# Low parts of the first weight quad: parts 1 and 2 subtracted on VectorE, parts 3 to 7 still made by an accumulating transfer

## The chip, the cores and the metric

The kernel runs on one core of a Trainium2 chip. The metric is device time in microseconds (us) of one execution, and the figure for the kernel before is the median of three runs: 1482.7 us (1477.24 to 1484.63). Beside these runs stands one profiled execution, from which every duration below is read.

A core has five engines that work at the same time, each through its own queue of instructions in order: TensorE (PE in the profile; PEld is its weight load), VectorE (DVE), ScalarE (ACT), GpSimd (POOL) and SyncE (SP). The last two only issue transfers here. An instruction that has to wait for another engine or for a transfer holds up everything behind it in its own queue.

## The reference

Two layers of an encoder over 512 positions of width 1024, in float32. Each layer has an attention half and a feed-forward half:

```python
for l in range(DEPTH):                        # DEPTH = 2
    h = rms_norm(x, attn_norm_g[l])
    z = jnp.einsum('bsd,dc->bsc', h, w_in[l])
    ...                                       # split, RoPE, two attention branches, gates
    x = x + jnp.einsum('bsd,de->bse', mixed, w_out[l])
    h = rms_norm(x, ffn_norm_g[l])
    u = jax.nn.silu(jnp.einsum('bsd,df->bsf', h, w_gate[l])) * jnp.einsum('bsd,df->bsf', h, w_up[l])
    x = x + jnp.einsum('bsf,fd->bsd', u, w_down[l])
```

The case lies in the feed-forward half: `w_gate` and `w_up` are 1024 x 2816, `w_down` is 2816 x 1024.

## The kernel before

**Numbers in two parts.** A float32 matrix is held as a rounded high part `h` (type fp32r) and a low part `lo = src - h`. A product takes three matmuls: high by high, high by low, low by high. So each operand of TensorE needs two preparations. ACT makes the high part (`A.copy`, in the profile CAST). The low part is made in one of two ways: VectorE subtracts (`V.tensor_tensor(..., ALU.subtract)`), or ACT writes `-h` (in the profile ACTIVATE) and POOL issues a transfer that adds the source to it (`accum_op=ALU.add`).

**The feed-forward half.** 256 columns of `w_gate` and `w_up` are taken straight (`pair_matmul`); the other 2560 go in five groups of 512 columns ("quads"), each quad as seven products of 512-row halves in place of eight (Strassen's scheme). A quad's source arrives as two raw tiles, `a11, a21` and `a12, a22`, each quarter 128 x 4 x 256. The seven parts are needed in the order 1, 5, 6, 2, 7, 3, 4 (`ORDER`, line 466). Part 1 is `a11`, part 2 is `a12`; parts 5, 6, 7 and 3 are sums that `Quad.high` makes on VectorE, most of them in place: for part 6 it overwrites `a21` and then `a11`, for part 3 it overwrites `a12`. The input has seven parts of the same kind, made once a layer by `chain_x` (lines 1360 to 1405): `high` on ACT, `low` on VectorE, and sums on VectorE between them.

**Where the first quad lies.** The first quad of `w_gate` of each layer (q = 0) is prepared early, while the last products with `w_out` and the straight columns still run. For it alone `by_transfer` is true (set in line 491, read in line 578): its seven low parts are made by ACT and POOL (`low_by_transfer`, lines 532 to 535). All later quads subtract on VectorE.

**One step of TensorE and what it needs.** `m_step` (line 1459) runs 24 matmuls of 256 columns for one part. After part 1, `seed` (line 1479) lets ACT copy the result to another bank; the matmuls of part 6 add to that bank, so TensorE can't begin part 6 before the copy is done. `evac_g` and `evac_u` (lines 1413 and 1419) take the straight columns out of the accumulators: VectorE scales, ACT applies SiLU, VectorE multiplies, ACT and VectorE split the result in two parts.

**What sets the order.** The kernel is planned before it is built: a dry pass walks through it with a clock per engine and estimated durations, and fixes the order in which each queue gets its instructions. Weight work falls due at positions counted in TensorE's time (`at_pos`, `tick`); other work stands in chains that are advanced when their operands are estimated to be ready (`Need`, `issue`). The same pass notes when each buffer is first and last used, and `Layout.pack` lays all buffers into two arenas (float32 and fp32r) so that buffers share room when their uses don't meet. An instruction that overwrites a buffer waits until everybody has read it, transfers included.

In the rows that follow `arena_72` is the float32 arena, `arena_73` the fp32r arena, `mm` and `at` are accumulator banks. Every instruction goes through one helper, so all have line 308 and are told apart by engine, operation, names and shape.

Of the kernel before, what the change touches and what calls it, by code (L numbers as in the profile page):

```python
# [213 lines left out]
def trunk(ctx: ExitStack, tc: tile.TileContext, a: dict, out: bass.AP, lay: Layout):  # L214
# [20 lines left out]
    def buf(shape, dtype=F32):  # L235

        n = int(np.prod(shape))
        x = lay.place(n, dtype)
        t = arenas[dtype][:, x : x + n]
        if len(shape) == 2:  # L240
            t = t.rearrange("p (a b) -> p a b", b=shape[1])
        elif len(shape) == 3:
            t = t.rearrange("p (a b c) -> p a b c", b=shape[1], c=shape[2])
        return t
# [287 lines left out]
    def low_by_transfer(lo, src, h):  # L532

        A.activation(lo, h.bitcast(F32), AF.Copy, scale=-1.0)
        GQ.dma_start(lo, src, accum_op=ALU.add)

    class Quad:
# [37 lines left out]
        def low(self, m):  # L575
            src, h = self.parts[m]
            lo = buf([4, 256], F32R)
            if self.by_transfer:
                low_by_transfer(lo, src, h)
            else:  # L580
                V.tensor_tensor(lo, src, h.bitcast(F32), ALU.subtract)
            self.parts[m] = h, lo
# [503 lines left out]
    def layer(l):  # L1086
# [273 lines left out]
        def chain_x():  # L1360
# [26 lines left out]
            high(1, b11)  # L1387
            V.tensor_tensor(n1, b11, b12, ALU.subtract)
            yield from low(1)
            high(5, n1)  # L1390
            yield from normal(1)
            V.scalar_tensor_tensor(n2, n1, -1.0, b22, ALU.mult, ALU.subtract)
            high(6, n2)
            yield from low(5)
            yield from low(6)
            high(2, b21)
            yield from low(2)
# [194 lines left out]
```

## Time and profile before

| | |
|---|---|
| median of 3 runs | 1482.7 us (1477.24 to 1484.63) |
| the profiled execution's own time | 1478.58 us |
| its span, first to last instruction | 1476.8 us |
| mean granted TensorE clock | 0.983 |
| busy, share of the span | PE 95%, DVE 62%, ACT 48%, POOL 25% |

A row of the timeline reads: start in us from the span's start, duration in us, engine, line, operation, output<-input with partitions x elements and types, how many such instructions follow each other, and in brackets the idle time of the engine just before it and what ended it. A row that joins several instructions shows the shape of the first. The view of waits adds up idle time by engine and releaser: total, how often, the longest. The chain of waits is followed back from the last instruction to what released it; "issue" is time in which the engine waited for nothing that the profile shows. In the table by windows, the value behind the busy times is the granted TensorE clock (1.00 is full), then the mean busy share of the DMA engines and GB/s.

### The profile page before, as it was taken

The page shows a single profiled execution, that of the slowest core. Times are in us where ns is not written, and L with a number is a line of the kernel's source. Part 1 is how long each engine was busy: PE and PEld are TensorE (multiplying, and loading weights), DVE is VectorE, ACT ScalarE, POOL GpSimd, SP SyncE. Part 2 cuts the span into 40 slices and gives each one's busy share as a digit, 9 for nine tenths or more (in the row PEclk, how much of TensorE's full clock was granted, in tenths as well). Part 3 has the DMA queues.
Part 4 walks back from the last instruction along what each step waited for, and adds up shares of the span by engine and source line. Part 5 has one row for each costly group of instructions (what it writes and reads, how often), then busy time and mean ns, then how long its engine had stood idle before and what let it go on. Part 6 is the DMA issues. An engine that isn't in the chain of part 4 may idle for free.

```text
span 1476.8 us, 21019 instructions
## 1 busy us (share of the span) xinstructions
PE 1405.2 (95%) x8074; PEld 1230.7 (83%) x8074; DVE 908.5 (62%) x1743; ACT 713.9 (48%) x1200; POOL 368.6 (25%) x374
## 2 busy tenths in 40 slices
PE   5999989999969999999999999999997999999998
PEld 4778878888869999999987887788886899999997
DVE  3876768543747565575647868673437575575653
ACT  3476657543544343433545775574345444343431
POOL 4533222234221110201353322123332211101111
PEclk9999999999989999999999999899999899999999
DMA  9877778899975745645798679669997754836455
GB/s 228 164 145 137 145 128 150 153 191 241 174 150 119 174 115 143 158 100 117 154 189 168 125 132 158 124 122 183 209 242 130 160 124 122 190 83 168 115 100 114
DMA packets 211427, 223.18 MB, mean 151 GB/s; under 512 B 25964, under 2 KB 179744, under 8 KB 211328
## 3 DMA queue, kind: packets, MB, share of 16 engines
q0 software_dynamic: 159920, 167.23, 61.1%
q1 hardware_dynamic: 51408, 54.62, 13.3%
q8 instruction: 63, 1.03, 0.3%
q14 instruction: 36, 0.29, 0.1%
HBM read 207.13 MB, written 2.10 MB: 142 GB/s over the span
## 4 chain that ended last, share of the span: by engine, by line
PE 69%; DMA 9%; DVE 9%; issue 7%; ACT 4%; POOL 2%; DVEq 0%; POOLq 0%; ACTq 0%; SPq 0%
PE mm L308 50%; PE at L308 19%; DVE arena L308 6%; ACT arena L308 4%; DMA arena<-arena 3%; DMA arena<-in_w_out 2%; DVE sm L308 2%; POOL arena L308 2%; DMA arena<-in_w_gate 1%; DMA arena<-in_w_up 1%; DMA arena<-in_rel_bias_b 1%; DMA vec<-in_q_norm_b 1%; DMA arena<-in_w_in 0%; ACT L308 0%; DVE hf L308 0%
## 5 line engine op out<-in xcount | busy, mean ns | idle before, releaser
L308 PE MATMUL mm<-arena 128*128 128x512 f32 (+1 forms) x5568 | 1127.9, 358 | 32.0 <-ACT mm L308 24.9
L308 PEld LDWEIGHTS mm<-arena 128*128 128x128 f32 x5568 | 910.1, 191 | 161.7 <-ACT mm L308 25.3
L308 PE MATMUL at<-arena 128*128 128x256 f32 (+2 forms) x1952 | 309.4, 299 | 15.1 <-DMA arena<-arena 12.3
L308 ACT ACTIVATE arena<-arena 128x1024 fp32r<-128x1024 f32 (+3 forms) x280 | 235.9, 865 | 176.9 <-DMA arena<-in_w_down 62.2
L308 ACT CAST arena<-arena 128x1024 fp32r<-128x1024 f32 (+2 forms) x250 | 211.7, 864 | 224.0 <-DVE arena L308 219.5
L308 PEld LDWEIGHTS at<-arena 128*128 128x128 f32 x1952 | 268.7, 193 | 38.7 <-DMA arena<-arena 11.9
L308 DVE TENSOR_TENSOR arena<-arena,arena 128x1024 fp32r<-128x1024 f32 (+2 forms) x236 | 228.3, 981 | 57.3 <-ACT arena L308 57.1
L308 POOL DMA_DIRECT2D arena<-in_w_in x168 | 168.4, 1367 | 368.3 <-ACT arena L308 367.9
L308 DVE TENSOR_TENSOR arena<-arena,mm 128x512 f32<-128x512 f32 x144 | 98.8, 686 | 255.9 <-PE mm L308 255.8
L308 POOL DMA_DIRECT2D arena<-in_w_down x96 | 98.2, 1210 | 503.2 <-ACT arena L308 388.4
L308 DVE TENSOR_TENSOR arena<-arena 128x1024 f32<-128x1024 f32 (+3 forms) x196 | 158.8, 824 | 19.2 <-DMA arena<-arena 14.1
L308 DVE TENSOR_TENSOR arena<-at,arena 128x384 fp32r<-128x384 f32 (+4 forms) x206 | 114.1, 562 | 52.7 <-ACT arena L308 45.9
L308 ACT CAST arena<-at 128x384 fp32r<-128x384 f32 (+2 forms) x164 | 74.4, 459 | 117.5 <-PE at L308 105.1
L308 PE MATMUL at<-cst,arena 128*128 128x128 f32 x504 | 87.4, 280 | 11.8 <-DVE arena L308 7.9
L308 PEld LDWEIGHTS at<-cst,arena 128*128 128x128 f32 x504 | 64.5, 143 | 30.5 <-DVE arena L308 10.9
L308 ACT ACTIVATE arena<-arena,negm 128x256 f32<-128x256 f32 (+1 forms) x128 | 71.6, 561 | 13.1 <-DVE negm L308 12.7
L308 DVE TENSOR_TENSOR arena<-mm,arena 128x512 f32<-128x512 f32 x72 | 49.3, 687 | 45.8 <-PE mm L308 45.7
L308 ACT COPY arena<-at 64x512 f32<-64x512 f32 (+1 forms) x60 | 34.8, 581 | 64.8 <-PE at L308 64.3
L308 POOL DMA_DIRECT2D arena<-in_w_out x32 | 35.2, 1292 | 54.5 <-ACT arena L308 54.5
L308 DVE CUSTOM_DVE_ANT_0 arena<-at,arena 128x256 f32<-128x256 f32 (+1 forms) x64 | 31.0, 486 | 28.7 <-PE at L308 28.4
L308 DVE CUSTOM_DVE_ANT_0 arena<-at,cst,nsnk 128x256 f32<-128x256 f32 (+1 forms) x64 | 34.3, 546 | 16.3 <-PE at L308 15.9
L308 DVE TENSOR_SCALAR arena<-arena,sm 128x384 f32<-128x384 f32 (+1 forms) x97 | 34.0, 405 | 1.1
(70 smaller groups left out, 444.2 us busy)
## 6 DMA issues: line engine op xcount, KB each, us to landing
arena<-in_w_in POOLq DMA_DIRECT2D x104, 512.0 KB, 7.1
arena<-in_w_down POOLq DMA_DIRECT2D x80, 512.0 KB, 6.8
arena<-in_w_gate SPq DMA_DIRECT2D x20, 1024.0 KB, 6.7
arena<-in_w_up SPq DMA_DIRECT2D x20, 1024.0 KB, 5.2
arena<-in_w_in POOLq DMA_DIRECT2D x64, 256.0 KB, 6.2
arena<-in_w_out POOLq DMA_DIRECT2D x32, 512.0 KB, 8.0
arena<-in_w_proj_a POOLq DMA_DIRECT2D x16, 512.0 KB, 8.8
arena<-in_w_proj_b POOLq DMA_DIRECT2D x16, 512.0 KB, 6.5
```

What stands on the lines that cost most here:

```text
L308: f(*args, **kw)
```

## The change

In `Quad.low` the two parts 1 and 2 of the first quad no longer go by transfer. They are subtracted by VectorE, as in all later quads. Parts 5, 6, 7, 3 and 4 of the first quad stay transfers. Part 1 and part 2 are the two whose source (`a11`, `a12`) a later sum overwrites.

```diff
         def low(self, m):
             src, h = self.parts[m]
             lo = buf([4, 256], F32R)
-            if self.by_transfer:
+            if self.by_transfer and m not in (1, 2):
                 low_by_transfer(lo, src, h)
             else:
                 V.tensor_tensor(lo, src, h.bitcast(F32), ALU.subtract)
             self.parts[m] = h, lo
```

Per layer that is two ACT instructions, two POOL transfers of 512 KB from buffer to buffer less, and two VectorE subtractions of 128 x 1024 more. The plan follows it in a few places of each layer. The orders of TensorE and SP stay the same from end to end; both arenas are packed anew.

VectorE's queue, first layer, from the second column of `evac_g` to the second of `evac_u`. Before: the sum of part 3 (`128x4x256`, the first of two) stands behind the low parts of the input's parts 5 and 6 (`x2`) and in front of the two columns of `evac_u`; the low part of the input's part 2 and the sum for its part 7 (the second `128x4x256`) stand between the two columns.

```order
L308 TENSOR_TENSOR arena_72<-mm_3282,arena_72 128x512
L308 TENSOR_TENSOR arena_73<-arena_72,arena_73 128x1024 x2
L308 TENSOR_TENSOR arena_72<-arena_72 128x4x256
L308 TENSOR_TENSOR arena_72<-mm_3392,arena_72 128x512
L308 TENSOR_TENSOR arena_72<-arena_72 128x512
L308 TENSOR_TENSOR arena_73<-arena_72,arena_73 128x512
L308 TENSOR_TENSOR arena_73<-arena_72,arena_73 128x1024
L308 TENSOR_TENSOR arena_72<-arena_72 128x4x256
L308 TENSOR_TENSOR arena_72<-mm_3393,arena_72 128x512
```

After: four subtractions follow each other (the weights' part 2, then the input's parts 5, 6 and 2), then two sums (the input's part 7, the weights' part 3), then both columns of `evac_u`.

```order
L308 TENSOR_TENSOR arena_72<-mm_3281,arena_72 128x512
L308 TENSOR_TENSOR arena_73<-arena_72,arena_73 128x1024 x4
L308 TENSOR_TENSOR arena_72<-arena_72 128x4x256 x2
L308 TENSOR_TENSOR arena_72<-mm_3391,arena_72 128x512
L308 TENSOR_TENSOR arena_72<-arena_72 128x512
L308 TENSOR_TENSOR arena_73<-arena_72,arena_73 128x512
L308 TENSOR_TENSOR arena_72<-mm_3392,arena_72 128x512
```

Moved forward are one subtraction and one sum of the input, which stood behind the sum of part 3 and now stand ahead of it; one subtraction is new.

ACT's queue at the same place, from the two SiLU of `evac_g`. Before: the third ACTIVATE is the negation of part 2; CAST x2 are the high parts of the weights' part 7 and the input's part 2; the copy to `mm` is `seed`, and right ahead of it stand the high parts of the weights' part 4 and of the input's part 3 (CAST x2).

```order
L308 ACTIVATE arena_72<-arena_72 128x512 x2
L308 ACTIVATE arena_73<-arena_73 128x1024
L308 CAST arena_73<-arena_72 128x1024 x2
L308 ACTIVATE arena_73<-arena_73 128x1024
L308 CAST arena_73<-arena_72 128x1024
L308 CAST arena_73<-arena_72 128x512
L308 ACTIVATE arena_73<-arena_73 128x1024
L308 CAST arena_73<-arena_72 128x1024
L308 CAST arena_73<-arena_72 128x512
L308 CAST arena_73<-arena_72 128x1024 x2
L308 COPY mm_3500<-at_3466 128x512
L308 ACTIVATE arena_73<-arena_73 128x1024
```

After: the negation of part 2 is gone, the input's part 7 is cast before the weights' part 3 (the second CAST x2), and the input's part 3 is cast behind `seed` and the negation of part 4.

```order
L308 ACTIVATE arena_72<-arena_72 128x512 x2
L308 CAST arena_73<-arena_72 128x1024 x2
L308 ACTIVATE arena_73<-arena_73 128x1024
L308 CAST arena_73<-arena_72 128x1024 x2
L308 CAST arena_73<-arena_72 128x512
L308 ACTIVATE arena_73<-arena_73 128x1024
L308 CAST arena_73<-arena_72 128x512
L308 CAST arena_73<-arena_72 128x1024
L308 COPY mm_3496<-at_3464 128x512
L308 ACTIVATE arena_73<-arena_73 128x1024
L308 CAST arena_73<-arena_72 128x1024
```

So one CAST of 128 x 1024 has moved from in front of `seed` to behind it, and one ACTIVATE of 128 x 1024 has left.

POOL's queue of transfers around the first quad's first parts, first layer, as a difference (`arena_73<-arena_72` are the accumulating transfers of low parts; `128x1024` is part 5, whose source is one piece).

```order
 L308 DMA arena_73<-in_w_up 128x4x256
 L308 DMA arena_73<-in_w_gate 128x4x256
-L308 DMA arena_73<-in_w_up 128x4x256 x2
-L308 DMA arena_73<-arena_72 128x4x256
-L308 DMA arena_73<-in_w_up 128x4x256
+L308 DMA arena_73<-in_w_up 128x4x256 x3
 L308 DMA arena_73<-arena_72 128x1024
-L308 DMA arena_73<-arena_72 128x4x256 x3
+L308 DMA arena_73<-arena_72 128x4x256 x2
 L308 DMA arena_73<-in_w_down 128x2x256
```

The transfer of part 1 has left between two slabs of `w_up`, and that of part 2 behind parts 5 and 6. In the second layer all three queues differ in the same way.

## The prediction

> **What bounds the kernel now.** I read the waits first, then the chain, then the timeline where they point. The waits, two rows of them:
>
> ```profile
> DVE arena L308 <- DMA arena<-arena: 14.1, 3, 7.0
> PE mm L308 <- ACT mm L308: 24.9, 2, 12.5
> ```
>
> TensorE is busy nearly all the time, and its largest loss is two waits, one a layer, for ACT's copy into an `mm` bank. VectorE has two waits of 7.0 us for a transfer from buffer to buffer. The chain in the first layer ties them together:
>
> ```profile
> 397.22 10.77 issue
> ...
> 408.00 5.50 DMA arena<-arena
> ...
> 413.53 1.84 DVE arena L308 x2
> ...
> 421.73 1.99 ACT arena L308 x2
> 423.74 0.58 ACT mm L308
> 424.36 5.49 PE mm L308 x24
> ...
> 472.87 5.76 PE at L308 x48
> ```
>
> The transfer of part 2's low part runs from 408.00 to 413.5; VectorE's sum for part 3 overwrites its source and starts as it lands; everything up to `seed` at 423.74 is queued behind; TensorE starts part 6 at 424.36. The timeline there, first layer:
>
> ```profile
> 406.06 5.91 PE L308 MATMUL at<-arena 128*128 128x256 f32 x48
> 424.36 5.49 PE L308 MATMUL mm<-arena 128*128 128x256 f32 x24 [12.39 <-ACT mm L308]
> 403.04 1.28 DVE L308 TENSOR_TENSOR arena<-mm,arena 128x512 f32<-128x512 f32 x2
> 404.23 2.35 DVE L308 TENSOR_TENSOR arena<-arena,arena 128x1024 fp32r<-128x1024 f32 x2
> 413.53 1.22 DVE L308 TENSOR_TENSOR arena<-arena 128x1024 f32<-128x1024 f32 x1 [6.94 <-DMA arena<-arena]
> 416.84 1.83 DVE L308 TENSOR_TENSOR arena<-arena,arena 128x512 fp32r<-128x512 f32 x2 [0.68 <-ACT arena L308]
> 418.58 1.22 DVE L308 TENSOR_TENSOR arena<-arena 128x1024 f32<-128x1024 f32 x1
> 405.52 2.10 ACT L308 ACTIVATE arena<-arena 128x512 f32<-128x512 f32 x3
> 407.53 1.98 ACT L308 CAST arena<-arena 128x1024 fp32r<-128x1024 f32 x2
> 408.00 1.28 POOL L308 DMA_DIRECT2D arena<-arena  x1 [10.78 <-ACT arena L308]
> ```
>
> TensorE ends parts 1 and 5 at 411.97 and stands 12.39 us. The negation of part 2 waits in ACT's queue behind the SiLU pair (it is the third of the x3), so its transfer is issued at 408.00 although its high part was cast long before. The second layer repeats it:
>
> ```profile
> 1147.95 5.49 PE L308 MATMUL mm<-arena 128*128 128x256 f32 x24 [12.50 <-ACT mm L308]
> 1127.79 2.35 DVE L308 TENSOR_TENSOR arena<-arena,arena 128x1024 fp32r<-128x1024 f32 x2
> 1137.12 1.23 DVE L308 TENSOR_TENSOR arena<-arena 128x1024 f32<-128x1024 f32 x1 [6.97 <-DMA arena<-arena]
> 1131.09 1.98 ACT L308 CAST arena<-arena 128x1024 fp32r<-128x1024 f32 x2
> ```
>
> **Part 2, first layer.** I walk the new order with the old durations. VectorE's 1024-wide operations start 1.13 apart (2.35 - 1.22). The new subtraction of part 2 takes the place at 404.23; the input's low parts 5 and 6 start at 405.4 and 406.5, VectorE is free at 407.6. Next is the input's low part 2, which needs ACT's second CAST of the pair 407.53 to 409.51. The negation ahead of that pair (as wide as one of the two casts in 1.98, so about 1.0 us) is gone, so the cast ends at 408.5. Low part at 408.5, the sum for the input's part 7 at 409.6, the sum for part 3 at 410.8. That is 2.7 us before 413.53, not 6.9: ACT's cast is what VectorE waits for next, 0.9 us, and two operations now stand ahead of the sum.
>
> From the sum to `seed` it was 423.74 - 413.53 = 10.2 us. Two 1024-wide operations have left that stretch (the second of the x2 at 416.84, and 418.58), 2.3 us; one CAST of the pair at 421.73 now stands behind `seed`, 1.0 us. So `seed` starts at 410.8 + 10.2 - 3.3 = 417.7 and TensorE, 0.62 behind it as before, at 418.3: 6.0 us earlier, in a hole of 6.4 where 12.4 stood. A gain of 6.0.
>
> **Part 2, second layer.** The pair of casts ends at 1133.07, less 1.0 is 1132.1; the sum for part 3 at 1132.1 + 2.3 = 1134.4, again 2.7 before 1137.12; with the same 3.3 another 6.0.
>
> **Part 1.** Its subtraction comes in front of the last residual sum of the attention half. The rows there:
>
> ```profile
> 381.36 1.03 ACT L308 CAST arena<-arena 128x1024 fp32r<-128x1024 f32 x1
> 382.43 1.06 ACT L308 ACTIVATE arena<-arena 128x1024 fp32r<-128x1024 f32 x1
> 382.60 0.69 DVE L308 TENSOR_TENSOR arena<-arena,mm 128x512 f32<-128x512 f32 x1 [2.03 <-PE mm L308]
> 384.14 0.75 DVE L308 SCALAR_TENSOR_TENSOR arena<-arena,vecT,arena 128x512 fp32r<-128x512 f32 x1 [0.85 <-ACT arena L308]
> 386.90 1.02 PE L308 MATMUL at<-ones,arena 128*128 128x1 f32 x8 [0.26 <-DVE arena L308]
> 392.21 1.23 DVE L308 TENSOR_TENSOR arena<-arena 128x1024 f32<-128x1024 f32 x1 [0.19 <-DMA arena<-arena]
> ```
>
> TensorE waits for this chain at 386.90, so a delay of VectorE would cost its full length. The subtraction runs from 382.4 to 383.6 and pushes the sum from 382.60 to 383.6; but what follows at 384.14 waited 0.85 us for ACT, and ACT, rid of the negation at 382.43, comes 1.0 us earlier. The next instruction starts at 384.2 instead of 384.14: cost 0 to 0.2 us a layer. The wait of 0.19 at 392.21 goes. I take the two as zero; if ACT's earlier start didn't help, 1.1 us a layer would be lost.
>
> **What leaves otherwise** (four negations, four transfers) had room: POOL's issue at 408.00 follows 10.78 us of idle time. Nothing there is on TensorE's path but the two waits above.
>
> **What is late next.** Behind part 6 TensorE needs parts 7, 3, a slab of `w_down`, part 4:
>
> ```profile
> 418.06 1.27 POOL L308 DMA_DIRECT2D arena<-arena  x1 [5.31 <-ACT arena L308]
> 425.65 1.26 POOL L308 DMA_DIRECT2D arena<-arena  x1 [6.32 <-ACT arena L308]
> 428.01 1.93 POOL L308 DMA_DIRECT2D arena<-in_w_down  x2 [1.09 <-ACT arena L308]
> arena<-arena POOLq DMA_DIRECT2D x14, 512.0 KB, 6.9
> ```
>
> The three issues (part 3, part 4, the slab) waited for ACT, whose work is the one that comes 6 us earlier, so they move with it. Part 4 lands at 425.65 - 6.0 + 6.9 = 426.6; TensorE comes to it four steps of about 2.9 us after 418.3, and part of that at a lower clock, not before 430. Covered. If these transfers didn't come earlier, the slab at 428.01 + 6.9 = 434.9 would be late by some 2 to 4 us.
>
> **The clock.** These windows are the hole, the 48 matmuls behind it, and for comparison a shorter hole earlier in the kernel with what follows it:
>
> ```profile
> 411.97:424.36 12.39, 0.00 (x1) 0.00 (x0) 9.21 (x11) 6.80 (x9) 2.06 (x3) 0.69 1.02 203
> 424.36:432.87 8.51, 8.51 (x49) 8.51 (x49) 3.57 (x4) 2.97 (x4) 3.20 (x3) 0.65 0.70 161
> 202.70:207.18 4.48, 0.31 (x2) 0.12 (x2) 0.09 (x1) 0.00 (x0) 0.00 (x0) 0.77 1.33 247
> 207.18:212.00 4.82, 4.82 (x14) 4.14 (x15) 1.33 (x5) 1.86 (x5) 0.00 (x0) 0.51 0.26 42
> ```
>
> After the hole 48 matmuls take 8.51 us, 5.76 at full clock (chain, 472.87): 2.75 us a layer go to the lower clock. A hole of 4.5 us was enough for it at 202.70, so one of 6.4 should be too: I take the loss as unchanged. [...]
>
> **The sum.** 2 x 6.0 = 12.0 us off the profiled execution, 1478.58 (span 1476.8 and 1.8 around it): 1466.6. That execution lies 4.1 under the median of the three runs, 1482.7, which would give 1470.7; the runs themselves spread over 7.4 us. I take 1469.5. One execution of this kernel can't tell less than about 0.5%, 7.4 us, from no change.
>
> **Rivals.**
> - *The next wait takes it back.* The transfers behind the hole are bound by DMA, not by their issue, and TensorE waits some 3.5 us a layer at the slab or at part 4. For it: the DMA share is 1.02 in the hole (203 GB/s). Against: it is 0.70 right behind, the issues wait for ACT, and two transfers less share the engines. Gain 2 x (6.0 - 3.5) = 5, time 1477.7, no difference to be told. Chance 0.13.
> - *The clock holds.* If the hole of 6.4 us doesn't lower it, 2 x 2.75 more: 1464 from the same base. Against it stands the row of 202.70. Chance 0.05.
> - *The new packing costs more than the wait* (slower). Both arenas are packed anew, so anywhere a slab's load may have to wait for a reader it didn't wait for before. Laying the new addresses over the old start and end times, I find one slab of `w_down` held up by 5.2 us, issued at
>
> ```profile
> 1225.00 0.77 POOL L308 DMA_DIRECT2D arena<-in_w_down  x1 [0.49 <-PE mm L308]
> 1251.40 1.05 ACT L308 ACTIVATE arena<-arena 128x1024 fp32r<-128x1024 f32 x1
> ```
>
>   The second row is its negation, 26 us behind the issue; less 5.2 and a landing of some 7 us that leaves 14, so it is covered. A load, a negation and an accumulating transfer in a row are some 15 us (6.9 + 1 + 6.9); from one such slab wholly uncovered the gain is gone, with two the time is 1482.7 - 12 + 30 = 1500. Chance 0.05.
> - *The edit doesn't do it*: the sum of part 3 still waits for a reader of `a12`. Its only other reader is ACT's cast, long over. 1482. Chance 0.02.
>
> **How the numbers follow.** The forecast has 0.75. Its own range: 10 to 13 us from the roundings of the walk and the part 1 bound, over runs that spread -5.5 to +1.9 around their median: 1464 to 1474. Reaching to the first rival up to 1477 and to the clock's at 1463 leaves under 2 in 10 outside. Faster by over 0.5%: 0.75 and the clock's 0.05, less 0.03 for runs that fall close to the bound, 0.77. Same: 0.13 + 0.02 + 0.02 of that, 0.17. Slower: 0.05 and 0.01 of the scatter, 0.06.
>
> **What the profile after would show.** VectorE's wait for `arena<-arena` falls from 14.1 us to next to nothing. TensorE's two waits for `seed` are 6.4 us each, 12.8 in place of 24.9; the sum of part 3 starts 2.7 us earlier against the end of TensorE's part 5, behind a short wait for ACT. The granted clock still falls there. The DMA wait at part 4 or at the first slab stays away. Wrong would be: a hole of more than 9 us, a TensorE wait for `in_w_down` behind it, or a new wait for a slab elsewhere.

## The result, and the profile after

| | before | after |
|---|---|---|
| median of 12 runs each, us | 1481.91 (1477.24 to 1486.5) | 1469.32 (1461.58 to 1477.62) |
| ratio, 95% interval | | 0.9915 (0.9893 to 0.9937) |
| TensorE's two waits for `seed`, us | 24.9 | 11.3 |
| VectorE's waits for `arena<-arena`, us | 14.1 | no such row |

The changed kernel is 12.6 us, 0.85%, faster. (Of all executions reported here one, of the kernel with the sum in a buffer of its own, is left out: it took 1558.27 us at a granted clock of 0.844.) Its waits on TensorE, the row that answers to the one shown of before, and two that could have taken the gain back (columns: total us, times, longest):

```profile
PE at L308 <- DMA arena<-arena: 16.5, 6, 5.0
PE at L308 <- DVE arena L308: 14.6, 19, 2.1
PE mm L308 <- ACT mm L308: 11.3, 2, 6.3
```

The two waits for `seed` are less than half of what they were. The other two rows were 12.3 and 12.5 us before; in this execution they are 4.2 and 2.1 us longer. Most of the first is one wait in the first layer's attention half, 4.26 us at 264.94, where before it is 0.78 us at 256.65; the second is mainly the wait at the feed-forward norm, taken up under part 1 below. The timeline of the first layer, the same place as in the prediction:

```profile
417.01 5.91 PE L308 MATMUL at<-arena 128*128 128x256 f32 x48
429.20 5.49 PE L308 MATMUL mm<-arena 128*128 128x256 f32 x24 [6.27 <-ACT mm L308]
413.82 1.28 DVE L308 TENSOR_TENSOR arena<-mm,arena 128x512 f32<-128x512 f32 x2
415.02 3.48 DVE L308 TENSOR_TENSOR arena<-arena,arena 128x1024 fp32r<-128x1024 f32 x3
419.38 1.23 DVE L308 TENSOR_TENSOR arena<-arena,arena 128x1024 fp32r<-128x1024 f32 x1 [0.87 <-ACT arena L308]
420.52 2.35 DVE L308 TENSOR_TENSOR arena<-arena 128x1024 f32<-128x1024 f32 x2
417.37 1.98 ACT L308 CAST arena<-arena 128x1024 fp32r<-128x1024 f32 x2
428.57 0.57 ACT L308 COPY mm<-at 128x512 f32<-128x512 f32 x1
```

TensorE ends parts 1 and 5 at 422.92 and stands 6.27 us. VectorE does three subtractions in a row (the new one of part 2, the input's 5 and 6), waits 0.87 us for ACT's pair of casts, and then makes the input's low part 2, the sum for its part 7 and the sum for the weights' part 3 (the second of the x2, from about 421.65). Where 6.94 us of waiting for a transfer stood, there is none.

TensorE's timeline in the second layer, and the clock behind both holes (windows: stretch, length, busy time of PE, PEld, DVE, ACT and POOL, then the granted clock, the DMA share and GB/s):

```profile
1147.67 5.12 PE L308 MATMUL mm<-arena 128*128 128x256 f32 x24 [5.04 <-ACT mm L308]
```

```profile
429.20:437.72 8.52, 8.52 (x48) 8.52 (x49) 3.18 (x4) 2.86 (x4) 3.20 (x3) 0.64 1.15 238
1147.60:1155.00 7.40, 7.33 (x44) 7.34 (x45) 2.44 (x4) 2.92 (x5) 3.19 (x3) 0.69 1.14 243
```

The 48 matmuls behind the first hole take 8.52 us, as long as before (8.51), so the shorter hole has given nothing of the clock back there.

The profiled execution needs one word of care. It is the slowest of the twelve, 1477.62 us, hardly under the 1478.58 of the profiled execution before, though its two holes are 12.4 - 6.3 and 12.5 - 5.0, together 13.6 us shorter. Most of it is lost ahead of the first hole, where this execution is 417.01 - 406.06 = 11 us later. But for part 1 the change moves no operation there; it packs the buffers anew, and whether that has a share is not shown. One of the stretches is the wait at 264.94, 3.5 us longer; another is the first norm. The timeline and the window of before:

```profile
45.38 1.02 PE L308 MATMUL at<-ones,arena 128*128 128x1 f32 x8 [2.06 <-DVE arena L308]
46.27 3.65 PE L308 MATMUL mm<-arena 128*128 128x512 f32 x15
```

```profile
46.00:52.00 6.00, 6.00 (x30) 4.79 (x30) 4.90 (x25) 4.47 (x8) 3.96 (x4) 1.00 0.49 63
```

The same of after:

```profile
46.05 1.63 PE L308 MATMUL at<-ones,arena 128*128 128x1 f32 x8 [2.14 <-DVE arena L308]
47.54 6.27 PE L308 MATMUL mm<-arena 128*128 128x512 f32 x15
```

```profile
46.30:53.10 6.80, 6.80 (x20) 5.64 (x21) 4.62 (x26) 2.26 (x5) 3.96 (x4) 0.50 0.48 66
```

The wait is the same 2.1 us, and the same 15 matmuls take 3.65 us at the full clock in one execution and 6.27 at half of it in the other. So a gain in two holes can't be read from two whole times of single executions; it is read from the holes, and from the medians.

### The profile page after: what moved, and what is told of

It reads as the page before. It is cut to its first block, busy times and chain, and to the rows that moved or that the text cites. A ratio compares the mean times of both kernels' runs of the same rounds, so it can differ in the third digit from the quotient of the medians.

```text
span 1475.8 us, 21001 instructions
## 1 busy us (share of the span) xinstructions
PE 1411.6 (96%) x8074; PEld 1235.8 (84%) x8074; DVE 913.0 (62%) x1747; ACT 711.8 (48%) x1196; POOL 363.6 (25%) x370
## 4 chain that ended last, share of the span: by engine, by line
PE 72%; DVE 8%; issue 7%; DMA 6%; ACT 4%; POOL 2%; SPq 0%; DVEq 0%; POOLq 0%; ACTq 0%
PE mm L308 55%; PE at L308 17%; DVE arena L308 7%; ACT arena L308 4%; DMA arena<-arena 2%; POOL arena L308 2%; DMA arena<-in_w_in 1%; DMA arena<-in_w_gate 1%; DVE sm L308 1%; DMA arena<-in_w_up 1%; DMA vec<-in_q_norm_b 1%; SPq L308 0%; DMA arena<-in_rel_bias_b 0%; ACT L308 0%; DVEq L1587 0%
## 5 line engine op out<-in xcount | busy, mean ns | idle before, releaser
L308 PE MATMUL mm<-arena 128*128 128x512 f32 (+1 forms) x5568 | 1133.0, 359 | 18.8 <-ACT mm L308 11.3
L308 ACT ACTIVATE arena<-arena 128x1024 fp32r<-128x1024 f32 (+3 forms) x276 | 232.2, 863 | 173.8 <-DMA arena<-in_w_down 58.9
L308 DVE TENSOR_TENSOR arena<-arena,arena 128x1024 fp32r<-128x1024 f32 (+2 forms) x240 | 233.0, 984 | 60.8 <-ACT arena L308 59.8
```

Source lines behind the costliest of these rows:

```text
L308: f(*args, **kw)
```

## The experiments

The theory: the gain is the wait of one in-place sum (weights' part 3, which overwrites `a12`) for the transfer that still reads `a12` (low part 2), with `seed` queued behind it on VectorE and ACT. All ratios are to the kernel before, in runs on the same chip.

**Part 2 alone.**

```diff
-            if self.by_transfer and m not in (1, 2):
+            if self.by_transfer and m != 2:
```

> Only part 2's low part goes to VectorE; part 1 stays a transfer. Theory (the in-place sum for part 3 waited for part 2's transfer): all of the change's gain is here. TensorE's two waits for `seed` are about 6.3 us each, VectorE's wait for `arena<-arena` is gone but for the 0.2 us of part 1, and the time is 12 to 13 us under the kernel before, 1469 to 1470. Rival (each negation and transfer that goes is worth the same, two of the four are left): 6 us, 1476.

Measured: 1469.37 us, ratio 0.991 (0.9884 to 0.9936): the whole gain. TensorE's waits for `seed`, then the timeline of the first hole and one row of VectorE in the second layer, then the clock behind the first hole:

```profile
PE mm L308 <- ACT mm L308: 13.5, 2, 7.2
```

```profile
419.96 4.70 PE L308 MATMUL mm<-arena 128*128 128x256 f32 x24 [6.31 <-ACT mm L308]
410.14 1.23 DVE L308 TENSOR_TENSOR arena<-arena,arena 128x1024 fp32r<-128x1024 f32 x1 [0.88 <-ACT arena L308]
1110.27 1.22 DVE L308 TENSOR_TENSOR arena<-arena 128x1024 f32<-128x1024 f32 x1 [0.96 <-DMA arena<-arena]
```

```profile
419.96:427.38 7.42, 7.42 (x49) 7.42 (x49) 2.88 (x4) 2.86 (x4) 3.19 (x3) 0.76 1.15 244
```

The first hole is the changed kernel's to a few hundredths, with VectorE's 0.88 us behind ACT in it; the second is 7.2 us, 0.9 more than expected. There the other in-place sum, that for part 6, which overwrites `a11`, waits 0.96 us for a transfer (1110.27), part 1's, and all that is queued behind it on VectorE comes as much later. It is the same mechanism, but small: part 1's transfer is nearly early enough. The rival, that each negation and transfer less is worth the same, falls.

**Part 1 alone.**

```diff
-            if self.by_transfer and m not in (1, 2):
+            if self.by_transfer and m != 1:
```

> Only part 1's low part goes to VectorE; part 2 stays a transfer. Theory: nothing, 1481 to 1484; the two waits for `seed` stay at 12.4 us each and VectorE waits 7 us a layer for part 2's transfer. The bound of the prediction for part 1 (VectorE 1.1 us later in the norm's chain, not made good by ACT) would be 2 us slower, 1484. Rival (each negation and transfer counts the same): 6 us faster, 1476.

Measured: 1478.64 us, ratio 0.9995 (0.9968 to 1.0022): no difference to be told. TensorE's waits, and VectorE's:

```profile
PE mm L308 <- ACT mm L308: 24.8, 2, 12.4
```

```profile
DVE arena L308 <- DMA arena<-arena: 13.8, 2, 7.0
```

Both holes and both waits of VectorE for the transfer are as before. Of three such waits before, the small one (0.19 us, part 1's) is gone, and nothing came of it that the time can tell. The interval is some 4 us each way, so the time alone doesn't exclude the prediction's bound of 2 us.

**As many transfers less, but two others.**

```diff
-            if self.by_transfer and m not in (1, 2):
+            if self.by_transfer and m not in (5, 6):
```

> Parts 5 and 6 go to VectorE in place of 1 and 2: as many negations and transfers leave as in the change, but part 2's transfer and the sum that overwrites its source stay. Theory: VectorE still waits several us a layer for `arena<-arena`; two subtractions of 1.15 us fall in VectorE's work ahead of the norm. The gain of 12 isn't there: 1478 to 1487. Rival (what helps is that ACT and the DMA queue have four negations and four transfers less, whichever they are): 1469 to 1471.

Measured: 1475.59 us, ratio 0.9958 (0.9935 to 0.9981). The gain of 12 isn't there, but the time lies under the expected range, and the theory's picture was wrong too: the wait for the transfer went, and so did half of the holes, and another wait came. TensorE's waits, and then VectorE's and POOL's timeline in the first layer:

```profile
PE mm L308 <- ACT mm L308: 12.4, 2, 6.4
PE at L308 <- DVE rstd L308: 9.3, 2, 5.6
```

```profile
389.79 1.23 DVE L308 TENSOR_TENSOR arena<-arena,arena 128x1024 fp32r<-128x1024 f32 x1 [1.18 <-ACT arena L308]
394.58 1.23 DVE L308 TENSOR_TENSOR arena<-arena,arena 128x1024 fp32r<-128x1024 f32 x1 [1.17 <-ACT arena L308]
403.75 1.26 POOL L308 DMA_DIRECT2D arena<-arena  x1 [13.93 <-ACT arena L308]
413.04 1.22 DVE L308 TENSOR_TENSOR arena<-arena 128x1024 f32<-128x1024 f32 x1
```

The two subtractions of parts 5 and 6 stand ahead of the norm's last step (389.79 and 394.58), the two sums for part 6 with them, and each subtraction waits 1.2 us for ACT's cast besides its own length. The norm comes later, TensorE waits for it (`rstd`, 9.3 us), and the planner, which sees a later norm, puts the SiLU pair ahead of the input's scaling: part 2's transfer starts at 403.75, and VectorE doesn't wait for it at the sum, 413.04. The saving of 12.5 in the holes less 9.3 at the norm is 3.2; the 0.42% measured is 6.2, with an interval of some 3.4 us each way; the difference was not taken apart. What this run shows for the theory is narrower than it was meant to: the transfer of part 2 costs nothing where it is early enough.

**The transfers kept, the overwriting taken away.**

```diff
+                self.s3 = buf([4, 256]) if self.by_transfer else self.a12
-                add(self.a12, self.a12, self.a11)
+                add(self.s3, self.a12, self.a11)
-            src = {1: self.a11, 2: self.a12, 3: self.a12, ...}[m]
+            src = {1: self.a11, 2: self.a12, 3: self.s3 if m == 3 else None, ...}[m]
```

> The kernel before with all seven low parts by transfer, but the sum for part 3 of that quad is written to a buffer of its own, so that it overwrites nothing. Theory: VectorE's wait for `arena<-arena` is gone with no low part moved, and TensorE's two waits for `seed` shrink. They don't shrink to 6.3 us: the negation of part 2 stays in ACT's queue (1.0 us) and the input's part 7 and one low part stay ahead of `seed`; 7.5 to 9.5 us each, 1473 to 1477. Rival (it is the work taken from ACT and the transfers, not the overwriting): no change, 1481 to 1484, the two waits at 12.4 us.

Measured: 1477.01 us, ratio 0.9963 (0.9939 to 0.9986). TensorE's waits for `seed`, then the timeline: the two holes, VectorE in the first of them, and one row of VectorE in the second.

```profile
PE mm L308 <- ACT mm L308: 18.6, 2, 9.9
```

```profile
431.08 5.02 PE L308 MATMUL mm<-arena 128*128 128x256 f32 x24 [8.62 <-ACT mm L308]
1149.27 4.40 PE L308 MATMUL mm<-arena 128*128 128x256 f32 x24 [9.94 <-ACT mm L308]
415.58 1.22 DVE L308 TENSOR_TENSOR arena<-arena 128x1024 f32<-128x1024 f32 x1
421.03 1.83 DVE L308 TENSOR_TENSOR arena<-arena,arena 128x512 fp32r<-128x512 f32 x2 [2.83 <-ACT arena L308]
426.43 0.69 DVE L308 TENSOR_TENSOR arena<-mm,arena 128x512 f32<-128x512 f32 x1 [2.43 <-issue]
1144.61 0.69 DVE L308 TENSOR_TENSOR arena<-mm,arena 128x512 f32<-128x512 f32 x1 [2.53 <-DMA arena<-arena]
```

No low part moved, the sum at 415.58 starts as soon as VectorE is free, and the holes shrink from 24.9 to 18.6 (the second, 9.94, is just above the expected 7.5 to 9.5). So the overwriting is what waited, and the rival (only the work taken from ACT and the transfers counts) falls. The time gains less than half of what the change gains, 5.5 us by the ratio.

The holes are 18.6 - 11.3 = 7.3 us longer than the changed kernel's, and most of that is another wait for a transfer. The order in the engines' queues is the one of before. The sum stands 8.4 us earlier against the end of TensorE's part 5 than before. Then VectorE waits 2.83 us for ACT, whose queue still has the negation of part 2, and, at the second column of `evac_u`, 2.43 us more, which the timeline puts down to "issue". In the second layer the same operation waits 2.53 us, and there the profile names the transfer that was issued behind part 2's, the low part of part 7; in the first layer VectorE's wait there is for the semaphore of that transfer too (issued at 419.84, 6.6 us before the wait ends). The operation has no operand in common with part 7. The likely reason, not shown, is that the arenas, packed anew for the added buffer, give its output room that the transfer still reads. Taking these two waits off the two holes, which is an estimate and no run, leaves 6.2 and 7.4 us, 13.6 in all, against 11.3 in the changed kernel and 13.5 with part 2 alone. By this estimate the overwriting alone, with the old order, accounts for about the whole gain in the holes; the run as it stands shows 24.9 - 18.6 = 6.3 us of it.

**All seven on VectorE.**

```diff
-            if self.by_transfer and m not in (1, 2):
+            if self.by_transfer and False:
```

> All seven low parts of the quad on VectorE. Theory: no transfer is left to wait for, but five more subtractions of 1.15 us a layer stand in VectorE's queue, those of 5 and 6 ahead of the norm's last step (2.3 us, which TensorE waits for) and that of 7 ahead of `seed` (1.15 us): 2 x 3.4 = 7 us of the 12 given back, 1474 to 1481. Rival (VectorE, at 62% busy, has room, and the fewer transfers the better): 1463 to 1469.

Measured: 1484.76 us, ratio 1.0041 (1.0021 to 1.006). Slower than before, and 4 us above the expected range. TensorE's waits:

```profile
PE at L308 <- DVE arena L308: 25.9, 19, 7.3
PE at L308 <- DVE rstd L308: 15.2, 2, 7.6
```

The holes at `seed` are gone and two others a layer have come: 7.6 us at the norm, and up to 7.3 at part 5, which waits for VectorE. At the norm the mechanism was the one expected and its price too low: only the subtractions were counted, 2.3 us, and not the casts that they wait for. VectorE's timeline there:

```profile
400.76 1.23 DVE L308 TENSOR_TENSOR arena<-arena,arena 128x1024 fp32r<-128x1024 f32 x1 [1.16 <-ACT arena L308]
401.90 2.48 DVE L308 TENSOR_TENSOR arena<-arena 128x1024 f32<-128x1024 f32 x2
405.54 1.23 DVE L308 TENSOR_TENSOR arena<-arena,arena 128x1024 fp32r<-128x1024 f32 x1 [1.17 <-ACT arena L308]
```

A negation and a transfer let VectorE go on; a subtraction right behind its cast waits 1.2 us for it. The two subtractions and their waits make 2 x 1.15 + 1.16 + 1.17 = 4.6 of the 7.6. Most of the rest are the two sums for part 6 (401.90, 2.48 us), which stand ahead of the norm's last step here and behind it before. The second hole stands at part 5 because the plan puts the low part of the input's part 5 behind both columns of `evac_u`: VectorE makes it from 431.74 to 432.96, and TensorE goes on at 433.01.

**What is left of the hole.** 6.3 us still stand in the changed kernel. VectorE's timeline in the changed kernel:

```profile
409.91 2.73 DVE L308 SCALAR_TENSOR_TENSOR arena<-arena,vecT 128x512 f32<-128x512 f32 x4
412.68 1.23 DVE L308 SCALAR_TENSOR_TENSOR arena<-arena 128x1024 f32<-128x1024 f32 x1
```

Four scalings of the input's second half and the sum behind them are put in its queue ahead of the gate pair's evacuation (413.82), because XLOG, the planner's bound on how far VectorE's queue may run ahead when the input's parts are put in it, allows 6.0 us of backlog.

```diff
-XLOG = 6.0
+XLOG = 2.6
```

> The change, and XLOG (how far VectorE's queue may run ahead when the normalised input's parts are put in it) from 6.0 to 2.6. By the order this puts the second half's four scalings and the sum behind them (2.73 and 1.23 us in the changed kernel's rows at 409.91 and 412.68) behind VectorE's evacuation of the gate pair, and the low parts of the input's parts 6, 2 and 7 behind `seed`. Theory (what is left of the hole, 6.3 us, is VectorE's and ACT's work queued ahead of `seed`): `seed` comes about 4 us earlier, the two waits for it are 1.5 to 3 us in place of 6.3, 7 to 9 us off the changed kernel; if a hole that short leaves the clock alone, up to 5.5 more. 1456 to 1463. Rival (the input's parts 6, 2 and 7, put off, are late now and TensorE waits for them instead): waits of VectorE's `arena` of 3 us or more behind `seed`, 1466 to 1471, no better than the change.

Measured: 1457.63 us, ratio 0.9849 (0.9827 to 0.9871): 22 us off the kernel before, about 10 off the changed one by the ratios. TensorE in both layers, and the clock behind the first hole:

```profile
419.83 3.33 PE L308 MATMUL mm<-arena 128*128 128x256 f32 x24 [1.96 <-ACT mm L308]
1129.28 3.34 PE L308 MATMUL mm<-arena 128*128 128x256 f32 x24 [1.96 <-ACT mm L308]
```

```profile
419.83:426.04 6.21, 6.21 (x49) 5.99 (x49) 4.08 (x5) 4.79 (x6) 3.21 (x3) 1.00 1.19 223
```

The two holes are 1.96 us each, 4.3 shorter, and in this execution the clock holds: 24 matmuls in 3.33 where 5.49 stood. Both terms of the expectation came. TensorE's waits for VectorE behind `seed` are 0.3 us, so the input parts that were put off are not late, and the rival falls.

**The same setting on the kernel before.**

```diff
-XLOG = 6.0
+XLOG = 2.6
```

> The kernel before (seven transfers) with XLOG from 6.0 to 2.6, no low part moved. By the order the SiLU pair, and with it part 2's negation and transfer, come some 4 us earlier and the sum for part 3 some 2 us later against them. Theory (the transfer costs only what it is late for the sum): VectorE's wait for `arena<-arena` falls from 7 us to 1 or less a layer, and TensorE's two waits for `seed` to 3 to 6 us; 1465 to 1470, as fast as the change without making it. Rival (a transfer that a sum must wait for is a cost wherever it stands): waits of 5 us or more stay, 1474 or more.

Measured: 1469.32 us, ratio 0.9913 (0.9887 to 0.9939), as fast as the change. The time is the expected one, the wait isn't (1 us or less was expected), and the first hole, 7.47 us, is above the expected 3 to 6; the timeline of both layers:

```profile
406.90 1.28 POOL L308 DMA_DIRECT2D arena<-arena  x1 [6.32 <-ACT arena L308]
413.74 1.23 DVE L308 TENSOR_TENSOR arena<-arena 128x1024 f32<-128x1024 f32 x1 [4.98 <-DMA arena<-arena]
422.42 4.52 PE L308 MATMUL mm<-arena 128*128 128x256 f32 x24 [7.47 <-ACT mm L308]
1132.66 1.23 DVE L308 TENSOR_TENSOR arena<-arena 128x1024 f32<-128x1024 f32 x1 [3.67 <-DMA arena<-arena]
1141.35 5.09 PE L308 MATMUL mm<-arena 128*128 128x256 f32 x24 [4.42 <-ACT mm L308]
```

The transfer does start earlier against TensorE (406.90, and TensorE ends part 5 at 414.95; before 408.00 and 411.97), but it takes 6.8 us, VectorE is at the sum at 408.76, and 5.0 and 3.7 us of the 7.0 remain. With the setting, the change is still worth some 9.5 us by the ratios (0.9913 to 0.9849). So the two gains are for the most part different ones: alone they are 12.6 and 12.9 us, together 22.3, where the sum would be 25.5; the intervals, over 3 us each, don't tell whether the difference is real.

**The setting with part 2 alone.**

```diff
-            if self.by_transfer and m not in (1, 2):
+            if self.by_transfer and m != 2:
-XLOG = 6.0
+XLOG = 2.6
```

> XLOG at 2.6 with part 2 alone on VectorE, part 1 a transfer again. Theory: part 1 is worth nothing here either, 1456 to 1459, the two waits for `seed` at 2 us each. Rival (with the shorter hole part 1's transfer, or the 1.1 us that its subtraction costs VectorE, shows): 1460 or more, or 1455 or less.

Measured: 1456.12 us, ratio 0.9837 (0.9804 to 0.9869), not to be told from the version with both parts: part 1 is worth nothing here either that the time can tell. Two things were not expected. The first hole is 0.75 us only, because TensorE comes to it later: behind the norm 15 matmuls take 5.30 us in this execution (its clock there is not shown) and 3.67 in the trace of before. The hole in the second layer is 1.96 us as with both parts, but here the clock fell behind it (timeline of both layers, window of the second).

```profile
414.51 3.33 PE L308 MATMUL mm<-arena 128*128 128x256 f32 x24 [0.75 <-ACT mm L308]
1125.56 4.76 PE L308 MATMUL mm<-arena 128*128 128x256 f32 x24 [1.96 <-ACT mm L308]
```

```profile
1125.56:1129.00 3.44, 3.44 (x15) 3.31 (x16) 1.82 (x3) 2.86 (x4) 1.94 (x2) 0.53 1.14 251
```

**Too far.**

```diff
-XLOG = 6.0
+XLOG = 2.0
```

> The change with XLOG at 2.0 in place of 2.6. By the order one thing more goes behind VectorE's evacuation of the up pair: the low part of the input's part 5, which TensorE needs before `seed`. Theory (VectorE's queue decides the hole, and putting input parts off pays until one that is needed early is late): TensorE waits 2 to 4.5 us a layer for VectorE at part 5, and a hole of that size lowers the clock in some executions; 1461 to 1467. Rival (what made XLOG 2.6 fast is only that less is queued ahead of `seed`, so still less is no worse): 1455 to 1458.

Measured: 1462.55 us, ratio 0.9877 (0.9846 to 0.9907), against 0.9849 at 2.6. TensorE's timeline in both layers:

```profile
414.15 5.28 PE L308 MATMUL at<-arena 128*128 128x256 f32 x23 [3.91 <-DVE arena L308]
1127.41 4.27 PE L308 MATMUL at<-arena 128*128 128x256 f32 x23 [3.93 <-DVE arena L308]
```

TensorE waits at part 5, for an input part that was put off too far, 3.9 us a layer in place of 1.96 at `seed`. The theory's price, place and time came. The intervals of the two ratios overlap, so it is by these waits, and not by the time, that the rival falls.

Of these, XLOG 2.6 with part 2 (and, to no difference, part 1) on VectorE beats both kernels: 0.985 of the time before, where the change has 0.9915.

## Why the prediction was right, step by step

- **Part 2, first layer.** Right. The predicted wait of VectorE for ACT, 0.9 us, is the row at 419.38 with 0.87. The sum for part 3 was predicted 2.7 us earlier: against the end of TensorE's part 5 it was 413.53 - 411.97 = 1.56 behind, and is 422.92 - 421.65 = 1.27 ahead, 2.8 earlier. From the sum to `seed` it is 428.57 - 421.65 = 6.9, as 10.2 - 3.3 has it. The hole is 6.27 where 6.4 was said. The three subtractions and the wait stand as walked. That the in-place sum's wait is the cause is shown by the run with a buffer of its own; how the gain divides between that wait and the order isn't: that run has another wait for a transfer, and without it, by the estimate given there, the old order would do about as well.
- **Part 2, second layer.** The saving was put at 6.0 again and is 7.5 in this execution, 5.3 with part 2 alone (7.2 us in place of 12.5). The operations are those of the first layer; what differs is how late TensorE comes to the hole (in the trace after, the norm's `rstd` is done at 401.83 and 1119.92, and part 5 ends 21.1 us later in the first layer and 22.7 in the second). These 1.6 us are the clock behind the norm: the same 15 matmuls take 3.67 us at 398.74 and 5.29 at 1116.83, with the granted clock at 0.50 from 1118.06 to 1121.47. So that the second hole is the shorter one, 5.04 us, is no gain of the change: TensorE spends the time ahead of it. With part 2 alone it is the longer one because of the wait for part 1's transfer, 0.96 us. The sum of the two holes was put at 12.8, and is 11.3 and 13.5 in the two executions.
- **Part 1.** Taken as zero, and zero as far as the times tell: alone it gives a ratio of 0.9995, and leaving it out changes nothing, at either setting of XLOG, to the 4 us or so that the times can tell. In the traces it isn't quite zero. Left a transfer it cost 0.96 us in one layer of one execution (1110.27 with part 2 alone). On the other side, in the trace after, TensorE's wait at the feed-forward norm is 1.36 and 0.93 us in the two layers, where it was 0.26 and 0.29. There VectorE's subtraction waited 2.94 us for ACT, whose work came behind the landing of a slab of `w_up`. With part 1 alone on VectorE the two waits are 0.73 and 0.80, with part 1 left a transfer 0.53 and 0.57, so of the difference at most some tenths of a us a layer are the subtraction's.
- **What leaves otherwise.** Right: two negations and two transfers less with part 1 alone bring nothing that the time can tell.
- **What is late next.** Right. Behind the holes (429 to 500 and 1147 to 1230) TensorE has no wait that the timeline marks; against the end of part 5 the transfer of part 4 and the slab are issued 6.2 and 7.1 us earlier, as said, that of part 3 only 2.8. The first rival, worth 0.13, did not come.
- **The clock.** Right where it was read: 48 matmuls in 8.52 us as before. (The hole at 202.70 that it was read from has 0.31 us of matmuls in its 4.48; the wait itself is 4.17.) It is less fixed than the prediction has it: in the second layer, behind 5.04 us, its two halves take 5.12 and 3.04 us where 5.49 and 3.38 stood; in the run with part 2 alone the 48 take 7.42 us behind a hole of 6.31; and behind 1.96 us nothing is lost in one execution and 1.4 (4.76 less 3.33) in another. These runs show no sharp bound in the length between a hole that costs and one that doesn't; the prediction used one that did, which was enough for 6.4.
- **The sum.** 12.0 us were predicted, 12.6 measured between the medians of twelve, 3.3 us either way. That the time came within 0.2 us of 1469.5 is luck: the two bases of the prediction gave 1466.6 and 1470.7, and the choice between them was not worked out.
- **The slower rival**, the new packing: no wait for a slab of `w_down` shows on TensorE in the trace after. It is excluded for this execution; what moved the rest of that trace (the first norm's clock above) is not shown to come from the new packing, and with part 2 alone on VectorE, a program packed anew too, the whole gain is there. A cost that is likely of this kind did come elsewhere, 2.5 us a layer in the run with a buffer of its own.

What the prediction did not see is the other side of its own term of 3.3 us: if taking two operations and a cast out of the stretch ahead of `seed` is worth 3.3 us, then what stands there still is the next thing to move. That was worth another 10 us.

## What to carry to other kernels

A transfer that only reads a buffer held up the sum that overwrites it by 6.9 and 7.0 us here; look for in-place sums behind a slow reader, and price the edit by the next wait in the same queue (here 2.8 us earlier, not the 6.9 that the wait was long) and by what is queued between the wait and the operation that the bounding engine needs. Moving an operation from a transfer to a busy engine is right only where its result or its place is urgent: one of seven brought everything, all seven lost it again at the norm and at part 5. A buffer of its own for the sum is the other remedy, and it has to be followed in the trace too, since it brought another wait for a transfer here (2.43 and 2.53 us; that the new layout is its cause is likely and not shown). When a hole has been halved, read its remainder by the same walk, since a queue that ran ahead of the urgent work was as good a cause here as a wait (4.3 us of the first hole's 6.3).

## What was not expected of the hardware

- Behind waits of the same length the clock fell in some executions and not in others: 2.06 us with the clock at 1.00 behind it and 2.14 us with 0.50 (the first norm, shown above), 1.96 us with 1.00 and with 0.53 (XLOG at 2.6 with both parts, and with part 2 alone). At the first norm with XLOG at 2.6 and both parts TensorE is idle for 2.06 us in all of the 4.20 from 42.50 to 46.70, as long as in the trace before, and there the clock is 0.50 from 46.70 to 50.10.
- In the traces of before and after all changes of the granted clock but those at the two ends lie whole multiples of 3.413 us apart. In the trace before it was 0.50 from 205.12 to 211.95 and from 416.75 to 430.40, which is 2 and 4 times that, and 1.00 for the 204.80 us between, 60 times; in the trace after it was 0.50 from 46.27 to 53.10, from 264.73 to 268.14 and from 425.15 to 435.39, 2 times, once and 3 times. What decides whether it falls behind a wait is not shown.
- So whether the clock falls behind a wait can be a cause of the spread between executions of one kernel (1461.58 to 1477.62 us after): at the first norm the same 15 matmuls took 3.65 us in the trace before and 6.27 in the trace after. That it is the only one is not shown; waits for transfers differ between executions as well (0.78 us at 256.65 before, 4.26 at 264.94 after).
- The transfer of 512 KB from buffer to buffer, part 2's, took 5.5 us from issue to the start of what waited for it before (408.00 to 413.53), and 6.8 in the kernel before with XLOG at 2.6 (406.90 to 413.74). Part 1's, as large, took 8.4 before (383.78 to 392.21). The price of a transfer that something waits for was a range of that width here.
